# First attention of a two-layer diffusion trunk: the squares' junk row moved to the closing tiles' row, the table of zeros made longer

## Chip, cores, metric

One core of a Trainium2 chip runs the whole program. The metric is the device time of one execution in microseconds (us), the median of several; lower is better. TensorE (PE) multiplies and transposes, VectorE (DVE), ScalarE (ACT) and GpSimd (POOL) do the elementwise work, and the SyncE queue (SP) issues nearly all DMA transfers, one after the other in a fixed order. SBUF is the on-chip memory: 128 partitions; a tile of `[128, 1024]` float32 takes 4096 bytes of each partition.

## What is computed

Two layers over 1024 latent tokens and 256 context tokens of width 1024. Layer 0 has a grouped-query attention and a recurrent mixer side by side, one output projection for both, then a ConvFFN; layer 1 has a neighbourhood attention and a ConvFFN. Cut to the parts that matter here:

```
# layer 0, mixer: q: 8 heads, k and v: 2 heads of 64; latent queries see 256 + 1024 keys, context queries 256
s = einsum("bqhgd,bkhd->bhgqk", q, k) * ATTN_SCALE
o = einsum("bhgqk,bkhd->bqhgd", softmax(s), v)
y = concat([o, readout(recurrent, gate)]) @ w_out            # 1024 x 1024
x = x + g1 * rms_norm(y, norm_post_mix)                      # the closing of a tile
h = rms_norm(x, norm_pre_ffn) * (1 + sc2) + sh2              # input of the ConvFFN
x = x + g2 * rms_norm(conv_ffn(h, w_up, conv_w, conv_b, w_down), norm_post_ffn)

def rms_norm(x, w): return x * rsqrt(mean(x * x) + EPS) * w
```

Everything is float32; a product is made of three matmuls of split operands (high and low parts, the `h`/`hi` and `l`/`lo` tiles).

## The kernel before

**The stage of the change** is `even_attention` (639 to 1061 us of the span): the attention, and in its gaps the output projection `project()`, which makes ten tiles of 128 tokens: two of the context, then eight latent ones. Its tiles live in the pool `at`, which lays them out from its bottom upward in the order in which they are first asked for: `zeros` (a column of zeros, 256 bytes), `pv_t` (1024 bytes), `sq_junk` (1024 bytes), the context keys `K2_0c`, three query tiles `a_q`, and so on; `y`, `y_x` and last of all `yjunk` (1024 bytes) lie at its top.

**The closing of a tile** is a list of small steps (`late`), of which one is taken after each group of three matmuls, or one after the other when no matmuls are left. For each half of the tile `y_half` (L351) squares the projection's PSUM bank on ACT, for the sum of squares alone (the squares themselves go into the junk row `yjunk` and are never read), and copies the bank to `y` on DVE. Then come `y_rstd` (DVE, DVE, POOL), `y_norm` and the sum with the old token values `y_x` (L1222, DVE), the store of `y` to `x1d` (L1224), `squares` (L1191: two ACT squares into the junk row `sq_junk`, again for the sums alone), another `y_rstd`, the scaling of `y` into `y_x` (L1229, ACT) and its store to `xnd` (L1230, issued by POOL). The old values for the next tile are loaded by L1216.

**The next stage** is the first ConvFFN's front (`up_front` in `ffn_up`, L1611 and on). SP there issues ten loads `n_x<-xnd` (512 KB each): the two context tiles, latent tiles 0 to 3, then two loads of the up-projection's weights (`w_raw<-in_w_up`, L1530), then latent tiles 4 to 7. The first `n_x` lies at the bottom of a new pool over the first 4096 bytes of `at`, and so over `zeros`, `pv_t`, `sq_junk`, `K2_0c` and the first `a_q`; the second and third lie above it. PE then transposes (L1344: eight context steps of two, then eight steps of four for tiles 0 to 3, later eight for tiles 4 to 7), ACT scales each step's bank (L1345, into `n_t` for the context and `x_t` after), and DVE splits the result (L1332 the high part, L1333 the low part). Between the sixth and the seventh context step ACT and POOL split the first block of weights (`w_A11h`, L1546, and `w_A11l`, L1547); after the eighth the second (`w_A12h`).

**What sets the order**: ACT, DVE, POOL, PE and SP keep the order in which the code stands (`in_order`), across both stages. SP stops at a load whose place in SBUF is still in use, and all loads behind it stand still too. A tile of a later pool waits for every instruction that used the bytes under it.

Of the kernel before, what the change touches and what calls it, by code (L numbers as in the profile page):

```python
# [11 lines left out]
F32 = mybir.dt.float32  # L12
F32R = mybir.dt.float32r
BF16 = mybir.dt.bfloat16
AF = mybir.ActivationFunctionType
# [5 lines left out]
P = 128  # L21
# [18 lines left out]
LINE = 32  # L40
# [25 lines left out]
class Trunk:  # L66
# [958 lines left out]
    def even_attention(self, gp, tp, pp, sp):  # L1025
# [5 lines left out]
        nc, a = self.nc, self.a  # L1031
# [155 lines left out]
                st["ready"] = b  # L1187

        def squares(y, ms):
            for h in range(2):  # L1190
                nc.scalar.activation(yjunk, y[:, 512 * h:512 * h + 512], AF.Square, scale=1.0 / 32.0, accum_out=ms[:, h:h + 1])  # L1191

        late = []

# [49 lines left out]
                elif late:  # L1244
                    late.pop(0)()

        zeros = sp.tile([P, 2 * LINE], F32, name="zeros", bufs=1)[:, 0:1]
        nc.vector.memset(zeros, 0.0)
        pv_t = sp.tile([P, QB], F32, name="pv_t", bufs=1)
        yjunk = sp.tile([P, 512], BF16, name="sq_junk", bufs=1)  # L1250
        N = 2 * len(pairs)
        later = {4: lambda: load_keys(0, 0), 6: lambda: load_keys(0, 1), 8: lambda: load_values(0, NT - 2),
                 10: lambda: load_keys(1, 0), 12: lambda: load_keys(1, 1), 14: lambda: load_gate(1)}
# [1614 lines left out]
```

## Time and profile before

| | us |
|---|---|
| median of 3 runs | 3322.68 |
| lowest, highest | 3320.38, 3323.68 |
| the profiled execution | 3321.63 |
| its span | 3319.9 |

The profile is one execution. Its page gives busy time by engine and the chain of work that ended last; the timeline gives single instructions with their start, their duration and, in brackets, how long the engine had been idle and for whom it waited. `SPq` marks the issue of a DMA by SP, `ACT`, `DVE`, `PE` and `POOL` the engines, `PEld` the weight loads of PE. In a row of windows stand the busy time of each engine, the clock that was granted to PE (PEclk, 1.00 is full), the mean share of time in which the DMA engines were busy, and the bytes moved.

### The profile page before, as it was taken

To read this page: it belongs to the slowest core of one execution; us is meant where nothing else is said; L and a number is where in the kernel's file an instruction comes from. 1 tells how busy PE (TensorE), PEld (TensorE's weight loads), DVE (VectorE), ACT (ScalarE), POOL (GpSimd) and SP (SyncE) were. 2 spreads that over 40 slices of the span, in tenths; PEclk is the share of its full clock that TensorE was granted. 3 is DMA by queue.
4 is the path that set the end of the run, shared out by engine and by line. 5 is a ranking of instruction groups with operands and counts; after the bars stand their busy time and mean duration, and the time that the engine had idled before them with its cause. 6 is when DMAs were issued, how large, how long until landed. Compare 5 with 4: busy or idle time off the path is not lost.

```text
span 3319.9 us, 48782 instructions
## 1 busy us (share of the span) xinstructions
PE 3097.1 (93%) x18364; PEld 2547.6 (77%) x18364; DVE 2019.6 (61%) x3386; ACT 1502.2 (45%) x2681; POOL 1562.5 (47%) x1181
## 2 busy tenths in 40 slices
PE   7989999789997899999999989999998989999997
PEld 4766777478886688888878768898986768888785
DVE  4366666567774654554577862477775555555778
ACT  3232232366664543343344442566665434434443
POOL 1130111487773566666510111677764367777202
PEclk8999999889998899999999989999998989999998
DMA  6534311721114121211385772222224212222856
GB/s 249 197 103 133 119 49 38 271 73 60 48 61 153 41 76 69 75 67 66 108 288 195 264 229 107 73 63 61 63 81 155 90 64 88 84 77 89 281 179 218
DMA packets 203357, 398.73 MB, mean 120 GB/s; under 512 B 23521, under 2 KB 85473, under 8 KB 203121
## 3 DMA queue, kind: packets, MB, share of 16 engines
q1 hardware_dynamic: 192512, 358.89, 32.1%
q0 software_dynamic: 10608, 36.72, 2.9%
q8 instruction: 144, 2.36, 0.3%
q14 instruction: 93, 0.75, 0.1%
HBM read 316.86 MB, written 79.06 MB: 119 GB/s over the span
## 4 chain that ended last, share of the span: by engine, by line
PE 72%; DVE 11%; ACT 3%; DMA 3%; issue 3%; POOL 2%; SPq 0%; POOLq 0%; DVEq 0%; ACTq 0%
PE g_ps L136 18%; PE u_g L136 14%; PE d_ps L136 11%; PE u_v L136 10%; PE u_pc L136 4%; PE a_pv L136 2%; PE c_pv L136 2%; PE c_s L136 2%; PE c_pt L2503 2%; PE a_pt L1136 2%; DVE a_pl L1138 1%; PE o_ps L136 1%; PE a_s L136 1%; ACT a_ph L1137 1%; DMA d_rawB<-in_w_down 1%
## 5 line engine op out<-in xcount | busy, mean ns | idle before, releaser
L144 POOL TENSOR_TENSOR rs_r<-rs_e,mhalf 128x1 f32<-128x1 f32 (+3 forms) x106 | 85.7, 809 | 855.7 <-DVE rs_e L143 805.7
L136 PE MATMUL d_ps<-d_Bl,d_Ah 128*128 128x512 f32 x704 | 276.7, 393 | 4.1 <-DVE d_Bl L1874 3.5
L136 PE MATMUL d_ps<-d_Bh,d_Ah 128*128 128x512 f32 x704 | 275.5, 391 | 2.8 <-ACT d_Ah L1873 1.8
L136 PE MATMUL d_ps<-d_Bh,d_Al 128*128 128x512 f32 x704 | 275.7, 392 | 2.0 <-DVE d_Al L1874 1.9
L2486 POOL TENSOR_SCALAR c_p<-c_p,rl 128x640 f32<-128x640 f32 (+1 forms) x128 | 232.5, 1818 | 95.4 <-DVE rl L2485 61.8
L1116 POOL TENSOR_SCALAR a_p<-a_p,rl 128x1280 f32<-128x1280 f32 (+1 forms) x80 | 240.3, 3007 | 55.8 <-DVE rl L1115 49.5
L136 PE MATMUL g_ps<-xh,w_hi 128*128 128x512 f32 (+1 forms) x640 | 256.7, 401 | 5.6 <-DVE hq L748 3.5
L136 PE MATMUL g_ps<-xh,w_lo 128*128 128x512 f32 (+1 forms) x640 | 237.5, 371 | 1.3 <-POOL w_lo L2386 1.3
L136 PE MATMUL g_ps<-xl,w_hi 128*128 128x512 f32 (+1 forms) x640 | 237.7, 371 | 0.0
L1138 DVE TENSOR_TENSOR a_pl<-a_pt,a_ph 128x512 fp32r<-128x512 f32 (+1 forms) x200 | 119.0, 602 | 95.6 <-ACT a_ph L1137 95.5
L1561 DVE TENSOR_TENSOR f_u<-u_v,f_p 128x512 f32<-128x512 f32 x88 | 60.5, 688 | 183.7 <-PE u_v L136 183.7
L1547 POOL TENSOR_TENSOR w_S4l<-w_s,w_S4h 128x512 fp32r<-128x512 f32 x44 | 57.2, 1299 | 229.7 <-ACT w_S4h L1546 229.7
L136 PEld LDWEIGHTS d_ps<-d_Bl,d_Ah 128*128 128x128 f32 x704 | 132.7, 188 | 36.7 <-DVE d_Bl L1874 8.6
L136 PEld LDWEIGHTS d_ps<-d_Bh,d_Ah 128*128 128x128 f32 x704 | 132.8, 189 | 32.6 <-ACT d_Ah L1873 3.1
L136 PEld LDWEIGHTS d_ps<-d_Bh,d_Al 128*128 128x128 f32 x704 | 132.9, 189 | 30.0 <-DVE d_Al L1874 3.3
L1137 ACT CAST a_ph<-a_pt 128x512 fp32r<-128x512 f32 (+1 forms) x200 | 102.0, 518 | 108.6 <-PE a_pt L1136 108.5
L2506 DVE TENSOR_TENSOR c_pl<-c_pt,c_ph 128x256 fp32r<-128x256 f32 (+1 forms) x256 | 112.9, 470 | 57.9 <-ACT c_ph L2505 56.8
L136 PE MATMUL g_ps<-w_hi,xh 128*128 128x512 f32 (+1 forms) x368 | 143.2, 389 | 4.7 <-DVE xh L2260 2.1
L136 PEld LDWEIGHTS g_ps<-xh,w_hi 128*128 128x128 f32 x640 | 121.4, 190 | 31.0 <-issue 14.3
L136 PE MATMUL g_ps<-w_lo,xh 128*128 128x512 f32 (+1 forms) x368 | 137.6, 374 | 4.1 <-DVE w_lo L2247 2.9
L2505 ACT CAST c_ph<-c_pt 128x256 fp32r<-128x256 f32 (+1 forms) x256 | 98.4, 414 | 91.6 <-PE c_pt L2503 89.5
L136 PEld LDWEIGHTS g_ps<-xh,w_lo 128*128 128x128 f32 x640 | 121.0, 189 | 24.1 <-POOL w_lo L2386 1.7
(570 smaller groups left out, 9902.6 us busy)
## 6 DMA issues: line engine op xcount, KB each, us to landing
m_raw<-in_w_mod SPq DMA_DIRECT2D x96, 512.0 KB
w_raw<-in_w_up SPq DMA_DIRECT2D x88, 512.0 KB
d_rawA<-actd SPq DMA_DIRECT2D x77, 512.0 KB
d_rawB<-in_w_down SPq DMA_DIRECT2D x74, 512.0 KB
actd<-f_t SPq DMA_DIRECT2D x22, 640.0 KB
d_t<-in_w_down SPq DMA_DIRECT2D x22, 512.0 KB
actd<-f_t SPq DMA_DIRECT2D x22, 512.0 KB
d_s<-actd SPq DMA_DIRECT2D x20, 512.0 KB
```

Source lines behind the costliest of these rows:

```text
L136: return self.nc.tensor.matmul(out, lhsT, rhs, start=start, stop=stop, skip_group_check=True, **k)
L144: nc.gpsimd.tensor_tensor(out=r[:p, :n], in0=e[:p, :n], in1=self.mhalf[:p, :n], op=OP.pow)
L1116: nc.gpsimd.tensor_scalar(Pt[:, :nk], Pt[:, :nk], rl, None, op0=OP.mult)
L1136: nc.tensor.transpose(pt[:, m, qt * P:(qt + 1) * P], Pt[:, kts[j + m] * P:(kts[j + m] + 1) * P], self.ident)
L1137: nc.scalar.copy(ph[:, j:j + n], pt[:, :n])
L1138: nc.vector.tensor_tensor(out=pl[:, j:j + n], in0=pt[:, :n], in1=ph[:, j:j + n].bitcast(F32), op=OP.subtract)
L1547: nc.gpsimd.tensor_tensor(out=lo, in0=part(j, name), in1=hi.bitcast(F32), op=OP.subtract)
L1561: nc.vector.tensor_tensor(out=out, in0=x, in1=y, op=OP.add)
L2486: nc.gpsimd.tensor_scalar(Pt[:, :n], Pt[:, :n], rl, None, op0=OP.mult)
L2503: nc.tensor.transpose(pt[:, j, :], Pt[:, (src + j) * P:(src + j + 1) * P], self.ident)
L2505: nc.scalar.copy(vap(ph, o, dims), pt[:, :cnt])
L2506: nc.vector.tensor_tensor(out=vap(pl, o, dims), in0=pt[:, :cnt], in1=vap(ph, o, dims).bitcast(F32), op=OP.subtract)
```

## The change

`squares` no longer has a junk row of its own. It asks for a tile named `yjunk` with one buffer, which is the tile that `y_half` uses, at the top of the pool. The tile `sq_junk` is gone (1024 bytes), and `zeros` grows from 256 to 768 bytes, of which only the first column is used, as before. So `pv_t` lies 512 bytes higher than it did and every tile from `K2_0c` on 512 bytes lower. Nothing else differs in the source.

```
         def squares(y, ms):
+            junk = sp.tile([P, 512], BF16, name="yjunk", bufs=1)
             for h in range(2):
-                nc.scalar.activation(yjunk, y[:, 512 * h:512 * h + 512], AF.Square, scale=1.0 / 32.0, accum_out=ms[:, h:h + 1])
+                nc.scalar.activation(junk, y[:, 512 * h:512 * h + 512], AF.Square, scale=1.0 / 32.0, accum_out=ms[:, h:h + 1])
...
-        zeros = sp.tile([P, 2 * LINE], F32, name="zeros", bufs=1)[:, 0:1]
+        zeros = sp.tile([P, 6 * LINE], F32, name="zeros", bufs=1)[:, 0:1]
         nc.vector.memset(zeros, 0.0)
         pv_t = sp.tile([P, QB], F32, name="pv_t", bufs=1)
-        yjunk = sp.tile([P, 512], BF16, name="sq_junk", bufs=1)
```

What it moves shows in the program's rows on two engines. On SP, at the seam of the two stages, the last load of old token values and the first loads of `n_x`, before (the names after "waits" are the semaphores: `DMAHW` and `DMASW` earlier DMAs, the others an engine):

```order
L1216 DMA y_x<-in_x 128x1024 [waits DMAHW7_49,DMASW7_49,Activation_49]
L1611 DMA n_x<-xnd 128x1024 [waits DMAHW0_49,DVE_49,Activation_49]
L1611 DMA n_x<-xnd 128x1024 [waits DMAHW1_49,PE_49]
L1611 DMA n_x<-xnd 128x1024 [waits DMAHW2_49,Pool_49]
L1611 DMA n_x<-xnd 128x1024 [waits DMAHW3_49]
```

and with the change:

```order
L1217 DMA y_x<-in_x 128x1024 [waits DMAHW7_49,DMASW7_49,Activation_49]
L1611 DMA n_x<-xnd 128x1024 [waits DMAHW0_49,DVE_49]
L1611 DMA n_x<-xnd 128x1024 [waits DMAHW1_49,PE_49]
L1611 DMA n_x<-xnd 128x1024 [waits DMAHW2_49,Pool_49]
L1611 DMA n_x<-xnd 128x1024 [waits DMAHW3_49]
```

The order is the same, and the first `n_x` no longer waits for ACT. On ACT, the closing of the last tile (`y_half` twice, then the squares twice, then the scaling), before:

```order
L354 ACTIVATE yjunk,y_ms<-g_ps 128x512 [waits PE_49]
L354 ACTIVATE yjunk,y_ms<-g_ps 128x512 [waits PE_49,Activation_49]
L1191 ACTIVATE sq_junk,y_ms<-y 128x512 [waits DVE_49]
L1191 ACTIVATE sq_junk,y_ms<-y 128x512 [waits Activation_49]
L1229 ACTIVATE y_x<-y,rs_r 128x1024 [waits DMAHW7_49,DMASW7_49,Pool_49]
```

and with the change:

```order
L354 ACTIVATE yjunk,y_ms<-g_ps 128x512 [waits PE_49,Activation_49] x2
L1192 ACTIVATE yjunk,y_ms<-y 128x512 [waits DVE_49,Activation_49]
L1192 ACTIVATE yjunk,y_ms<-y 128x512 [waits Activation_49]
L1230 ACTIVATE y_x<-y,rs_r 128x1024 [waits DMAHW7_49,DMASW7_49,Pool_49]
```

The squares and the first half of a tile now also wait for the ACT instruction that last wrote the shared junk row; over the whole stage nine such waits are added.

## The prediction

> **What bounds the kernel now.** The page comes first: the span, PE's busy share and the chain that ended last.
>
> ```profile
> span 3319.9 us, 48782 instructions
> PE 3097.1 (93%) x18364; PEld 2547.6 (77%) x18364; DVE 2019.6 (61%) x3386; ACT 1502.2 (45%) x2681; POOL 1562.5 (47%) x1181
> PE 72%; DVE 11%; ACT 3%; DMA 3%; issue 3%; POOL 2%; SPq 0%; POOLq 0%; DVEq 0%; ACTq 0%
> ```
>
> PE bounds most of the program; 28% of the chain are seams, where PE stands still for something else. A change that touches only two junk squares per tile and some addresses can matter only at such a seam, so the windows of the attention, of the projection's rest and of the seam behind it come next (us; busy time of PE, PEld, DVE, ACT and POOL with counts; PEclk; DMA share; GB/s):
>
> ```profile
> 639.00:1027.00 388.00, 343.23 (x2124) 294.65 (x2125) 269.08 (x536) 256.90 (x506) 300.94 (x153) 0.96 0.21 72
> 1027.00:1053.00 26.00, 25.76 (x114) 20.99 (x112) 10.05 (x18) 10.48 (x27) 8.64 (x14) 1.00 0.36 135
> 1053.00:1074.00 21.00, 6.37 (x20) 3.21 (x20) 7.78 (x19) 7.26 (x15) 2.37 (x5) 0.59 0.73 265
> ```
>
> From 1027 to 1053 PE is full and the DMA engines are nearly two thirds idle. Then come 21 us in which PE works for 6.4 and the DMA engines are the busy ones. The timeline tells why the transfers come so late:
>
> ```profile
> 1043.18 0.33 SPq L1216 DMA_DIRECT2D y_x<-in_x  x1
> 1058.61 0.63 ACT L1191 ACTIVATE sq_junk<-y 128x512 bf16<-128x512 f32 x1
> 1059.14 0.19 ACT L1191 ACTIVATION_READ_ACCUMULATOR sq_junk<-y 128x1 f32 x1
> 1059.36 3.03 SPq L1611 DMA_DIRECT2D n_x<-xnd  x6
> 1062.49 1.05 SPq L1530 DMA_DIRECT2D w_raw<-in_w_up  x2
> 1063.58 6.88 SPq L1611 DMA_DIRECT2D n_x<-xnd  x4
> ```
>
> SP issues nothing from 1043.51 (1043.18 + 0.33) to 1059.36, and starts 0.03 us after the last square of the last tile has ended (1059.14 + 0.19). The first `n_x` holds a context tile, whose values were written long before; it waits only because it lies over `sq_junk`. ACT shows what this costs:
>
> ```profile
> 1060.45 1.15 ACT L1229 ACTIVATE y_x<-y,rs_r 128x1024 f32<-128x1024 f32 x1 [1.12 <-POOL rs_r L144]
> 1065.23 0.56 ACT L1345 ACTIVATE n_t<-n_pv,mod,mod 128x256 f32<-128x256 f32 x1 [3.63 <-PE n_pv L1344]
> 1065.70 0.56 ACT L1345 ACTIVATE n_t<-n_pc,mod,mod 128x256 f32<-128x256 f32 x1
> 1068.83 0.56 ACT L1345 ACTIVATE n_t<-n_pt,mod,mod 128x256 f32<-128x256 f32 x1
> 1073.16 0.62 ACT L1546 CAST w_A11h<-w_raw 128x512 fp32r<-128x512 f32 x1 [3.77 <-DMA w_raw<-in_w_up]
> 1073.69 0.56 ACT L1345 ACTIVATE n_t<-n_pv,mod,mod 128x256 f32<-128x256 f32 x1
> ```
>
> ACT stands still twice: 3.63 us for the first transposes, which wait for `n_x`, and 3.77 us for the weights, which stand behind six `n_x` in SP's order. The chain from there on has no transfer in it (start, us, what):
>
> ```profile
> 1062.49 10.65 DMA w_raw<-in_w_up
> 1073.69 0.57 ACT n_t L1345
> 1074.28 1.02 DVE x_ctx3h L1332
> ...
> 1085.18 1.58 DVE x_B211l L1333
> ...
> 1086.81 1.81 PE u_g L136 x5
> ```
>
> After 1073.69 DVE's splits set the pace until PE's first long products.
>
> **The change, part by part.** *The wait that goes.* The first `n_x` keeps a wait for DVE, an earlier DMA and, one row on, PE and POOL. Which DVE work lies under it follows from its neighbours, `zeros` and `pv_t`:
>
> ```profile
> L1103 DVE CUSTOM_DVE_ANT_0 a_p<-a_s,zeros x64: 1462/1492/1494, 673.0 to 999.4; 128x1280 f32<-128x1280 f32 x64
> L1172 DVE TENSOR_TENSOR a_oT<-a_pv,pv_t x36: 416/417/419, 653.4 to 1027.3; 64x256 f32<-64x256 f32 x36
> ```
>
> The last reader of `zeros` starts at 999.4 and that of `pv_t` at 1027.3. The attention's PE and POOL work on keys, queries and probabilities is over by then too (its last value product feeds that L1172). So the first `n_x` can go as soon as SP is free, at 1043.5, 15.9 us earlier; six take 3.03 us to issue, until 1046.5.
>
> *Whether they arrive in time.* What the DMA engines move at most, and what else they carry there:
>
> ```profile
> 1070.00:1080.00 10.00, 6.61 (x30) 5.14 (x29) 5.76 (x10) 6.78 (x12) 2.54 (x2) 0.63 1.02 409
> xnd<-y_x POOLq DMA_DIRECT2D x3, 512.0 KB, 3.0
> x1d<-y POOLq DMA_DIRECT2D x2, 512.0 KB, 3.0
> ```
>
> The last two rows are of 1040 to 1085. At 409 GB/s 512 KB (0.524 MB) take 1.28 us, one transfer alone 3.0 from issue to landing. One `y_x`, six `n_x` and at most three stores are ten: 12.8 us, all down by 1056.5. The last `y_x` is the first among them, and the sum that reads it stands behind the last projection product. The two weight loads stay behind that product:
>
> ```profile
> 1052.38 0.39 PE L136 MATMUL g_ps<-w_hi,a_ol 128*128 128x512 f32 x1
> 1063.20 0.45 PE L1344 MATMUL n_pv<-ident,n_x 128*128 128x128 f32 x1 [10.44 <-DMA n_x<-xnd]
> ```
>
> They are issued at 1052.8, with `n_x` 4 and 5 and the last-but-one store about them: five transfers, 6.4 us, plus 3.0: landed by 1062.2 at the worst. The last `n_x` waits for the store of the last tile, as before (the scaling that feeds it ends at 1061.6); it is read only behind the products that began at 1086.81.
>
> *What ACT then does.* PE transposes three context steps into its three free banks while the last tile is closed. ACT, in order, reaches the first one when the scaling ends: 1060.45 + 1.15 = 1061.6. First gain: 3.63 us. Five steps on, at 1068.83 - 3.63 + 0.47 (the spacing of two steps) = 1065.7, it wants the weights, which landed 3.5 us earlier or more. Second gain: 3.77 us. Sum: 7.4; since instructions of ACT that follow each other without a gap overlap by some 0.1 (1065.23 + 0.56 to 1065.70), 7.4 to 7.6. I take 7.5. DVE's splits then start from step seven as in the rows above, at the same distances, and the whole of what follows moves with them.
>
> *Whether it is kept.* Behind the front PE is full and the DMA engines are not, so nothing later holds a fixed time:
>
> ```profile
> 1140.00:1160.00 20.00, 20.00 (x101) 16.98 (x101) 11.16 (x14) 9.47 (x14) 13.28 (x10) 1.00 0.08 34
> 1200.00:1300.00 100.00, 100.00 (x533) 86.61 (x532) 49.07 (x56) 39.67 (x57) 65.53 (x49) 1.00 0.19 69
> ```
>
> *The waits that are added* are between ACT's own instructions, which are in order anyway. The pair L1191 already has such a wait. Nine are added; at 0.2 us each (the accumulator read of 0.19 that would have to end first) they cost 1.8 us of ACT at the most, in a stretch where ACT is busy 10.5 of 26 us and waits for DVE or PE. I take nothing; without that cover only the last tile's two, 0.4 us, would be on the path. *The longer table* is cleared in one column as before and no other row of the stage's start changes: nothing. *The shifted addresses*: the 64 softmax instructions L1103 on six buffers take 1462 to 1494 ns, 2% apart; but those buffers lie 5120 bytes apart, so no row shows a shift of 512. I take nothing, bound by 1% either way over the attention's 388 us, 3.9 us.
>
> The profiled execution: 3321.63 - 7.5 = 3314.1. It stood 1.05 below the median of the runs; the median becomes 3322.68 - 7.5 = **3315.2 us**.
>
> **The rivals.** *A: as worked out*, gain 6.5 to 8.5: 3314.2 to 3316.2.
>
> *B: the clock takes a part back.* PE's granted clock was at half through the gap and rose just before the first products:
>
> ```profile
> 1076.00:1078.00 2.00, 1.82 (x11) 1.59 (x10) 1.93 (x5) 1.97 (x4) 0.56 (x1) 0.65 1.03 412
> 1078.00:1080.00 2.00, 2.00 (x11) 1.56 (x11) 1.97 (x4) 1.97 (x4) 0.00 (x0) 1.00 1.00 377
> 1078.96 0.39 PE L136 MATMUL u_g<-x_B110h,w_A11l 128*128 128x512 f32 x1
> 1079.19 0.39 PE L136 MATMUL u_g<-x_B110h,w_A11h 128*128 128x512 f32 x1
> 1129.64 0.63 PE L136 MATMUL u_v<-x_T40h,w_A22h 128*128 128x512 f32 x1
> 1130.07 0.63 PE L136 MATMUL u_v<-x_T40l,w_A22h 128*128 128x512 f32 x1
> ```
>
> A product starts every 0.23 us at full and every 0.43 at half clock. If the clock rises only after the first twelve, they cost 12 x 0.20 = 2.4 us, and the gain is 5.1: 3317.6. For it: the rise came after about 3 us of dense transposes, which the change moves. Against it: the transposes ahead of them close up too. The Trainium skill (TensorE: Matmul & The Clock Gate, Part 1) says that the clock is judged in free-running windows of about 3.4 us; by that rule the rise may fall up to a window later or earlier, which would make this rival, or its mirror F, a matter of phase. The half clock agrees with the rows; the window no row here can show.
>
> *C: only the first gap closes.* If the weights still came late (SP stopped at one of the rows ahead of them), the gain is 3.6: 3319.1. Against it: 3.5 us to spare.
>
> *D: it doesn't do what it says.* If another wait of the first `n_x` ends as late as the squares, nothing moves: 3322.7. The readers above speak against it.
>
> *E: slower.* The new addresses slow the attention's instructions, which are near PE's pace (343 of 388 us). It turns the sign from 7.5 / 388 = 1.9% on; at 3% it costs 11.6, less the 7.5: 3326.8. The evenness of L1103 speaks against it, as far as it reaches.
>
> *F: more.* A later stretch of half clock (the products at 1129 above are one) closes up with the shift; twelve products at 0.20 bring 2.4 more, two such stretches 4: 3311.2 to 3312.8.
>
> **How the numbers follow.** A 0.67, B 0.12, C 0.07, D 0.04, E 0.05, F 0.05. The predicted time is A's, 3315.2. The range is 3311.2 to 3319.8: it holds A, B, C and F and leaves D and E (0.09) and some scatter out. A measurement of this kernel tells 0.2% from no change, 6.6 us, so 3316.0 is the border. Faster: F and nine tenths of A, 0.65. Same: the rest of A, B, C and D, 0.30. Slower: E, 0.05.
>
> **What would show it.** In the changed profile: six `n_x` issued from about 1043.5, right behind the last `y_x`; the weights at about 1053; the first `n_t` within 0.1 us of the end of the last scaling, at 1061.6; no idle time before `w_A11h`; the products `u_g` that began at 1086.81 at about 1079.3; everything from 1140 on 7.5 us earlier. The attention up to 1027 should stand unmoved within 1 us; if it does not, E or its opposite is at work. A `w_raw` that lands after 1065.7 would make C right, an SP that still waits until 1059 D.

## The result, and the profile after

| kernel | median us | lowest to highest | runs | ratio to before (95%) |
|---|---|---|---|---|
| before | 3323.89 | 3317.06 to 3329.13 | 12 | |
| the change | 3316.61 | 3310.89 to 3321.46 | 12 | 0.9978 (0.9970 to 0.9986) |

The change is faster by 7.3 us (3323.89 - 3316.61), with an interval of 4.7 to 10.0 us (0.0014 and 0.0030 of 3323.89). The forecast was a gain of 7.5. The profiled execution took 3318.7 us. The page's first lines after:

```profile
span 3316.9 us, 48786 instructions
PE 3101.1 (93%) x18364; PEld 2548.8 (77%) x18364; DVE 2018.7 (61%) x3386; ACT 1501.4 (45%) x2681; POOL 1560.2 (47%) x1181
PE 73%; DVE 11%; DMA 3%; ACT 3%; issue 3%; POOL 1%; SPq 0%; DVEq 0%; POOLq 0%; ACTq 0%
```

The two spans differ by only 3.0 us, less than the medians do. Single executions of one kernel lie 10.6 to 12.1 us apart here, so spans of one execution each can't carry the result, and neither can a time of day in the trace. What can be compared is a distance between two landmarks that lie close together. The one used below, called the seam, runs from the start of the last tile's scaling (L1229, now L1230) to the start of the product `u_g<-x_B211l,w_A12h`, the first of the five with which the prediction's chain ended.

The timeline of SP after (start, duration, queue, line, what; a row holds equal issues that follow each other):

```profile
1034.53 11.60 SPq L1217 DMA_DIRECT2D y_x<-in_x  x2
1046.22 2.83 SPq L1611 DMA_DIRECT2D n_x<-xnd  x6
1055.36 0.87 SPq L1530 DMA_DIRECT2D w_raw<-in_w_up  x2
```

The six `n_x` go 0.09 us after the last `y_x` has been issued (1034.53 + 11.60 = 1046.13), no longer after the last square. SP is done with them at 1049.05 and issues the weights at 1055.36, 9.1 us behind the first `n_x`; before it was 3.1 (1062.49 - 1059.36). The timelines of ACT and of PE's first product of the five:

```profile
1063.07 1.15 ACT L1230 ACTIVATE y_x<-y,rs_r 128x1024 f32<-128x1024 f32 x1 [1.11 <-POOL rs_r L144]
1064.13 0.55 ACT L1345 ACTIVATE n_t<-n_pv,mod,mod 128x256 f32<-128x256 f32 x1
...
1067.70 0.56 ACT L1345 ACTIVATE n_t<-n_pt,mod,mod 128x256 f32<-128x256 f32 x1
1068.17 0.61 ACT L1546 CAST w_A11h<-w_raw 128x512 fp32r<-128x512 f32 x1
1068.68 0.56 ACT L1345 ACTIVATE n_t<-n_pv,mod,mod 128x256 f32<-128x256 f32 x1
```

```profile
1064.73 0.69 PE L1344 MATMUL n_pv<-ident,n_x 128*128 128x128 f32 x2 [6.95 <-ACT n_t L1345]
1081.85 0.50 PE L136 MATMUL u_g<-x_B211l,w_A12h 128*128 128x512 f32 x1 [1.17 <-DVE x_B211l L1333]
```

Both idle times of ACT (3.63 and 3.77 us) are gone: the first `n_t` starts as the scaling ends, and `w_A11h` follows the sixth `n_t` without a pause. The seam was 1086.81 - 1060.45 = 26.36 us and is 1081.85 - 1063.07 = 18.78: shorter by 7.58. PE now stands ready with its first context steps and waits 6.95 us for ACT, which is held by the closing of the last tile. The window ahead of the seam (busy time of PE, PEld, DVE, ACT, POOL; PEclk; DMA share; GB/s):

```profile
1046.00:1056.00 10.00, 9.33 (x42) 7.39 (x40) 3.70 (x7) 3.75 (x9) 2.24 (x4) 1.00 0.87 326
```

The transfers that waited behind the last square now lie beside PE's last projection products: a DMA share of 0.87 while PE works 9.33 of 10 us. The chain that ended last has no transfer left at the seam:

```profile
1059.16 1.24 DVE y L1223
...
1063.07 1.15 ACT y_x L1230
1064.22 0.46 ACT n_t L1345
...
1069.28 1.08 DVE x_ctx3h L1332
...
1080.22 1.58 DVE x_B211l L1333
1081.85 1.43 PE u_g L136 x5
```

Where it went through `w_raw` for 10.65 us, it now goes through the last tile's closing and ACT's context steps. That is what is late next.

### The profile page after: what moved, and what is told of

The parts are those of the page before. It is cut to its first block, busy times and chain, and to the rows that moved or that the text cites. A ratio compares the mean times of both kernels' runs of the same rounds, so it can differ in the third digit from the quotient of the medians.

```text
span 3316.9 us, 48786 instructions
## 1 busy us (share of the span) xinstructions
PE 3101.1 (93%) x18364; PEld 2548.8 (77%) x18364; DVE 2018.7 (61%) x3386; ACT 1501.4 (45%) x2681; POOL 1560.2 (47%) x1181
## 4 chain that ended last, share of the span: by engine, by line
PE 73%; DVE 11%; DMA 3%; ACT 3%; issue 3%; POOL 1%; SPq 0%; DVEq 0%; POOLq 0%; ACTq 0%
PE g_ps L136 18%; PE u_g L136 14%; PE d_ps L136 11%; PE u_v L136 11%; PE u_pc L136 4%; PE a_pv L136 2%; PE c_pv L136 2%; PE c_s L136 2%; PE c_pt L2503 2%; PE a_pt L1136 2%; DVE a_pl L1138 1%; PE a_s L136 1%; PE o_ps L136 1%; DMA m_raw<-in_w_mod 1%; ACT a_ph L1137 1%
## 5 line engine op out<-in xcount | busy, mean ns | idle before, releaser
L2486 POOL TENSOR_SCALAR c_p<-c_p,rl 128x640 f32<-128x640 f32 (+1 forms) x128 | 232.2, 1815 | 96.0 <-DVE rl L2485 63.1
```

Source lines behind the costliest of these rows:

```text
L2486: nc.gpsimd.tensor_scalar(Pt[:, :n], Pt[:, :n], rl, None, op0=OP.mult)
```

## The experiments

**The change again.** The same kernel, timed and profiled a second time beside the others.

> The changed kernel once more, beside the others. Wait theory (the first n_x no longer waits for the last squares): 7.5 us faster than before (7.4 of ACT's idle time at the seam), with the six n_x issued right behind the last y_x. Address theory (the tiles' places 512 bytes off make the stage itself faster): 7.5 us faster too, but the attention ends earlier and not the seam. Chance: nothing above 3 us.

Median 3316.37 us over 11 runs, ratio 0.9983 (0.9974 to 0.9991). The span was 3319.0, yet the seam is 1083.84 - 1065.06 = 18.78 us, the same to 0.01. Where no engine waits for a transfer, a seam of one trace can thus be read to a few hundredths of a microsecond, a span only to several. A seam with such waits was not traced twice.

**Wait back: the wait returns, the addresses stay.** On the changed kernel, the squares' junk goes to `pv_t`, which lies at the pool's bottom as `sq_junk` did. No tile moves.

```
         def squares(y, ms):
-            junk = sp.tile([P, 512], BF16, name="yjunk", bufs=1)
+            junk = pv_t.bitcast(BF16)
```

> All tiles lie as in the change, but the squares' junk goes into the bytes of pv_t, which lie under the first n_x: the wait for the last squares is back. Wait theory: the 7.5 us are gone, within 2 us of before; SP issues its first n_x within 0.1 us of the end of the last squares, and ACT is idle some 3.6 us and 3.8 us again. Address theory: 7.5 us faster, as the change.

Median 3321.64, ratio 1.0006 (0.9997 to 1.0016): the gain is gone. SP, ACT and PE of this kernel:

```profile
1064.39 0.19 ACT L1192 ACTIVATION_READ_ACCUMULATOR pv_t<-y 128x1 f32 x1
1064.60 3.19 SPq L1611 DMA_DIRECT2D n_x<-xnd  x6
1065.70 1.15 ACT L1230 ACTIVATE y_x<-y,rs_r 128x1024 f32<-128x1024 f32 x1 [1.12 <-POOL rs_r L144]
1070.38 0.56 ACT L1345 ACTIVATE n_t<-n_pv,mod,mod 128x256 f32<-128x256 f32 x1 [3.53 <-PE n_pv L1344]
1078.74 0.62 ACT L1546 CAST w_A11h<-w_raw 128x512 fp32r<-128x512 f32 x1 [4.20 <-DMA w_raw<-in_w_up]
1092.40 0.50 PE L136 MATMUL u_g<-x_B211l,w_A12h 128*128 128x512 f32 x1 [1.18 <-DVE x_B211l L1333]
```

SP starts 0.02 us after the last square (1064.39 + 0.19) again, and both idle times of ACT are back. The seam is 1092.40 - 1065.70 = 26.70. The wait alone makes the gain; the 512 bytes by which tiles moved make none that shows. That this seam is 0.34 longer than before's lies in the two idle times, which together are 0.33 longer (3.53 + 4.20 against 3.63 + 3.77).

**Sixth waits: round the wait in another way.** On the kernel before, `sq_junk` stays where it was, but the load that lies over it is the sixth in SP's order, not the first; nothing of the attention is touched.

```
-            tags = dict(zip((8, 9, 0, 1, 2, 3, 4, 5, 6, 7), ["x_T" + x for x in ("20h", "20l", "21h", "21l", "30h", "30l")] +
+            tags = dict(zip((8, 9, 0, 1, 2, 3, 4, 5, 6, 7), ["x_T" + x for x in ("20l", "21h", "21l", "30h", "30l", "20h")] +
                             ["x_T1" + x for x in ("0h", "0l", "1h", "1l")]))
+            xs[3] = hp.tile([P, D], F32, name="n_x", tag=tags[3], bufs=1)
...
-                    xs[i] = hp.tile([P, D], F32, name="n_x", tag=t, bufs=1)
+                    if i != 3:
+                        xs[i] = hp.tile([P, D], F32, name="n_x", tag=t, bufs=1)
```

> The kernel before, its junk row at the bottom and all of the attention's addresses untouched; only the first n_x in SP's order and the sixth (latent tile 3) trade places, so that the sixth lies over the junk row and waits for the squares. Wait theory: five n_x are issued behind the last y_x, both of ACT's idle gaps close (the weights are issued about 1060, land by 1064 and are wanted at 1065.7 of the span of before), 6 to 7.5 us faster. Address theory: within 2 us of before.

Median 3315.81, ratio 0.9979 (0.9970 to 0.9988): all of the gain, without the change.

```profile
1051.79 16.07 SPq L1613 DMA_DIRECT2D n_x<-xnd  x6
1067.97 1.15 SPq L1530 DMA_DIRECT2D w_raw<-in_w_up  x2
1068.65 1.15 ACT L1229 ACTIVATE y_x<-y,rs_r 128x1024 f32<-128x1024 f32 x1 [1.12 <-POOL rs_r L144]
...
1073.74 0.61 ACT L1546 CAST w_A11h<-w_raw 128x512 fp32r<-128x512 f32 x1
1087.42 0.50 PE L136 MATMUL u_g<-x_B211l,w_A12h 128*128 128x512 f32 x1 [1.18 <-DVE x_B211l L1333]
```

The row of six issues is 16.07 us long because its last one waits for the squares, and the weights behind it go only at 1067.97, 7.0 us later against the scaling than with the change (0.7 us ahead of it, not 7.7). Still the seam is 18.77. Five loads went ahead of the wait, and the weights are there when ACT gets to them at 1073.74, 5.8 us after their issue; before, they took 10.65 with six `n_x` beside them. The wait for the squares stands unchanged in this kernel and costs nothing: what cost was that six loads and the weights stood behind it together.

**Each gap alone.** *Weights first*, on the kernel before: both weight loads ahead of all ten `n_x`, everything still behind the squares' wait but the weights.

```
             with self.in_order(mybir.EngineType.SP):
+                load(0, 0)
+                load(0, 1)
                 for i, t in tags.items():
-                    if i == 4:
-                        load(0, 0)
-                        load(0, 1)
```

*Weights last*, on the changed kernel: the loads are free of the squares, and the weights go behind all ten `n_x`.

```
                 for i, t in tags.items():
-                    if i == 4:
-                        load(0, 0)
-                        load(0, 1)
                     xs[i] = hp.tile([P, D], F32, name="n_x", tag=t, bufs=1)
                     nc.sync.dma_start(xs[i], self.xnd[i * P:(i + 1) * P])
+                load(0, 0)
+                load(0, 1)
```

Both put the third weight load, `load(1, 0)`, and its pool behind these by hand, so that it keeps its place.

> The kernel before, but the two weight loads stand ahead of the n_x in SP's order, so that they go when PE's last projection product ends (1052.8) while the n_x still wait for the squares. Wait theory, with two gaps of their own: the first gap stays (3.6 us idle before the first n_t), the second (3.77 before w_A11h) closes: 3 to 4 us faster than before. If the two gaps were one and the same wait, 0 or 7.5.

> The change, but the two weight loads stand behind all ten n_x in SP's order, and so behind the last one, which waits for the store of the last tile. Wait theory with two gaps: the first gap stays closed, ACT is idle again before w_A11h, by about 5 us (weights issued some 6.5 us after the last scaling starts, 3 us to land, wanted 5.1 us after it): 2 to 4 us faster than before. If it is the first gap alone that counts, 7.5; if the second alone, nothing.

Weights first: 3319.04, ratio 0.9994 (0.9985 to 1.0003). Weights last: 3319.93, ratio 0.9997 (0.9988 to 1.0006). Neither can be told from no change by its time, and the interval of each holds the gain that its seam shows; the traces are sharper. Weights first:

```profile
1063.45 1.15 ACT L1229 ACTIVATE y_x<-y,rs_r 128x1024 f32<-128x1024 f32 x1 [1.12 <-POOL rs_r L144]
1069.04 0.56 ACT L1345 ACTIVATE n_t<-n_pv,mod,mod 128x256 f32<-128x256 f32 x1 [4.43 <-PE n_pv L1344]
1073.10 0.61 ACT L1546 CAST w_A11h<-w_raw 128x512 fp32r<-128x512 f32 x1
1086.93 0.50 PE L136 MATMUL u_g<-x_B211l,w_A12h 128*128 128x512 f32 x1 [1.18 <-DVE x_B211l L1333]
```

Weights last:

```profile
1060.28 1.15 ACT L1230 ACTIVATE y_x<-y,rs_r 128x1024 f32<-128x1024 f32 x1 [1.12 <-POOL rs_r L144]
1061.34 0.55 ACT L1345 ACTIVATE n_t<-n_pv,mod,mod 128x256 f32<-128x256 f32 x1
1069.80 0.62 ACT L1546 CAST w_A11h<-w_raw 128x512 fp32r<-128x512 f32 x1 [4.32 <-DMA w_raw<-in_w_up]
1083.47 0.51 PE L136 MATMUL u_g<-x_B211l,w_A12h 128*128 128x512 f32 x1 [1.18 <-DVE x_B211l L1333]
```

Each has exactly one of the two idle times: 4.43 us for the first context step, or 4.32 for the weights. The seams are 1086.93 - 1063.45 = 23.48 and 1083.47 - 1060.28 = 23.19, gains of 2.88 and 3.17 against before. Together that is 6.05, less than 7.58, because in either kernel the gap that stays is longer than it was (4.43 against 3.63, 4.32 against 3.77). In weights last that is SP's order: the last `n_x` waits for the last tile's store, and the weights behind it are issued 5.05 us after the scaling's start (1065.33 - 1060.28) and need 4.44 us to land. In weights first PE gets the second context tile 6.16 us after the first `n_x` is issued (1068.52 - 1062.36), where before it took 5.36 (1064.72 - 1059.36); why it lands later was not found.

**Junk only: the junk row moved, the table left short.** On the changed kernel `zeros` goes back to 256 bytes.

```
-        zeros = sp.tile([P, 6 * LINE], F32, name="zeros", bufs=1)[:, 0:1]
+        zeros = sp.tile([P, 2 * LINE], F32, name="zeros", bufs=1)[:, 0:1]
```

> The change without the longer table: the junk row is shared, zeros stays at 256 bytes, and every tile from K2_0c on lies 1024 bytes lower than before, so that K2_0c reaches over the modulation tables that DVE finishes at 637.5 of the span of before; its load then waits for DVE, where it went at 625.6. Wait theory: the seam gains 7.5 as in the change, the start loses some 2 us (the load lands about 3 us after 637.5, so the first scores come at 640.6 and not by 639.6, and the query loads behind it on SP's queue are late too): 4 to 6 us faster than before. If the longer table is worth nothing, 7.5.

Median 3321.31, ratio 0.9992 (0.9983 to 1.0001): by the ratio 2.7 us faster, with an interval from 0.3 slower to 5.6 faster. The seam is that of the change, 1085.06 - 1066.27 = 18.79, so 7.57 us are won there. Part of it is lost where the stage starts:

```profile
639.61 1.26 DVE L339 SCALAR_TENSOR_TENSOR mod<-mod,nrm 128x16 f32<-128x16 f32 x1
640.90 0.38 SPq L1070 DMA_DIRECT2D K_0c<-k2d  x1
...
679.43 1.49 DVE L1103 CUSTOM_DVE_ANT_0 a_p<-a_s,zeros 128x1280 f32<-128x1280 f32 x1
...
1066.27 1.15 ACT L1230 ACTIVATE y_x<-y,rs_r 128x1024 f32<-128x1024 f32 x1 [1.12 <-POOL rs_r L144]
1085.06 0.50 PE L136 MATMUL u_g<-x_B211l,w_A12h 128*128 128x512 f32 x1 [1.18 <-DVE x_B211l L1333]
```

The same rows of the kernel before:

```profile
625.56 0.42 SPq L1070 DMA_DIRECT2D K_0c<-k2d  x1
636.13 1.41 DVE L339 SCALAR_TENSOR_TENSOR mod<-mod,nrm 128x16 f32<-128x16 f32 x1
...
672.99 1.49 DVE L1103 CUSTOM_DVE_ANT_0 a_p<-a_s,zeros 128x1280 f32<-128x1280 f32 x1 [1.03 <-PE a_s L136]
```

The load of the first keys used to be issued 10.57 us ahead of L339, the last instruction of the modulation. Now it goes 0.03 us after L339 has ended (639.61 + 1.26). With 1024 bytes less at the bottom, `K2_0c` begins at byte 21376 of a partition, and the modulation's tiles end at 21696; with the change it begins at 21888. In the built program the load waits for DVE in this kernel, and neither before nor with the change. From L339 to the first long softmax instruction the kernel before takes 36.86 us, this one 39.82: 3.0 us lost. In the six other runs it is 36.7 to 37.2 us, so the loss is known to some tenths. The net, 7.57 - 2.96 = 4.6, lies inside the interval of the medians, which alone would not tell it from no change. The longer table is thus no part of the gain; it keeps the freed bytes from opening the same kind of wait at the stage's other end.

**Not tried.** What is late now is the closing of the last tile, ahead of ACT's context steps; `xnd` of that tile is needed only much later. Putting the context steps ahead of the closing would use PE's 6.95 us, but both stages would need their SBUF and PSUM at once, and no kernel of that kind was run.

## Why the prediction was right

**The wait that goes.** Right: the six loads follow the last `y_x` by 0.09 us. Wait back shows that the squares' junk was what held them, so D (it doesn't do what it says) is out. The issue came at 1046.22, 16.85 us ahead of the scaling where the prediction had 1060.45 - 1043.5 = 16.95; the trace as a whole stood later.

**Whether they arrive.** Right: neither ACT nor PE waits for a transfer from the scaling to the five products. The weights were issued 1063.07 - 1055.36 = 7.7 us ahead of the scaling, as forecast (1060.45 - 1052.8 = 7.65). The trace's landing records put the first weights at 1061.6, and ACT takes them at 1068.17: 6.5 us to spare, so C (only the first gap closes) was further off than the forecast 3.5 us said. The step ahead of that was a little short: the sixth `n_x` landed at 1059.9, where the forecast had all ten transfers down by 1056.5, which is 1059.1 in this trace (its scaling starts 2.62 us later). Nothing waited for it. In sixth waits the weights landed 0.7 us before ACT took them, and that was still in time.

**What ACT then does.** Right in both terms and in the sum: 7.4 to 7.6 forecast for the seam, 7.58 measured, 7.3 (4.7 to 10.0) in the medians. The two gaps as separate terms held only because both closed; a gap that is left alone grows by 0.6 to 0.8 us, as the pair of experiments shows.

**Whether it is kept.** The medians keep it. From the scaling to the first store of the next part (`actd`) the trace of the change gains more than 7.58:

```profile
L1595 SPq DMA_DIRECT2D actd<-f_t x1: 326/326/326, 1143.8 to 1143.8; - x1
```

That is 80.73 us after the scaling; before it was 89.45 (1149.9 - 1060.45). So 8.7 us by then, 1.1 more than at the product. This 1.1 is not the removed wait's. Wait back, which has the wait, takes 62.0 us from the product to the store (1154.4 - 1092.40), like the change (1143.8 - 1081.85); before took 63.1. In the trace of before PE's granted clock was 0.50 from 1088 to 1090, right behind the product, and the five products took 1.81 us; in the change and in wait back it was 1.00 there, and they took 1.43. So F (more) is not shown as an effect of the change: the half clock was absent with the wait as well.

**The rival B was priced without its cover.** In the changed kernel's trace the clock rose before the first product, as before. In wait back it did not:

```profile
1085.28 0.63 PE L136 MATMUL u_g<-x_B110h,w_A11l 128*128 128x512 f32 x1
1085.71 0.52 PE L136 MATMUL u_g<-x_B110h,w_A11h 128*128 128x512 f32 x1
1086.07 0.39 PE L136 MATMUL u_g<-x_B110l,w_A11h 128*128 128x512 f32 x1
```

The third and fourth product start 0.43 us apart (1085.28 to 1085.71) where 0.23 is the distance at full clock; only from 1086.07 on does one take 0.39 again. Weights last has four slow products too. They delay PE by about 0.8 us (4 x 0.20), and at the seam's end they cost nothing: from `w_A11h` to the product `u_g<-x_B211l` it is 13.66 us in wait back (1092.40 - 1078.74) and 13.67 in weights last, against 13.65 before and 13.68 in the change. DVE's splits, which set the pace at full clock, cover the delay. But that cover was used up. In wait back the chain that ended last runs through PE's twelve products:

```profile
1084.63 3.44 PE u_g L136 x12
```

From there it goes over ACT's `x_t` to the split `x_B211h`, where in the change it stays on DVE's splits. So only a third of what B supposed was seen, four slow products of twelve, and that was just covered. What twelve would have cost no run shows.

**What was costed at nothing.** The nine added waits of ACT cost nothing that shows:

```profile
1060.48 0.63 ACT L1192 ACTIVATE yjunk<-y 128x512 bf16<-128x512 f32 x1 [4.37 <-DVE y L1223]
1061.23 0.63 ACT L1192 ACTIVATE yjunk<-y 128x512 bf16<-128x512 f32 x1
```

The two squares start 0.75 us apart, as before (1057.86 and 1058.61). The shifted addresses cost nothing either: the 64 long softmax instructions keep their pace,

```profile
L1103 DVE CUSTOM_DVE_ANT_0 a_p<-a_s,zeros x64: 1464/1492/1493, 676.1 to 1002.0; 128x1280 f32<-128x1280 f32 x64
L1172 DVE TENSOR_TENSOR a_oT<-a_pv,pv_t x36: 416/417/420, 656.3 to 1029.9; 64x256 f32<-64x256 f32 x36
```

and from the first of them to the last reader of `pv_t` the attention takes 1029.9 - 676.1 = 353.8 us, against 1027.3 - 673.0 = 354.3. That ends E. The longer table was rightly costed at nothing against the kernel before. The prediction did not ask what would have happened without it: 3.0 us.

**What it called for and did not get**: an attention that stands still within 1 us up to 1027, and everything from 1140 on 7.5 us earlier. This trace runs 3.0 us late at the end of the modulation and 2.6 at the last scaling, ahead of anything that the change shortens, and its lead over the trace of before shrinks to 3.0 us at the end. As tests these were badly chosen, since they compare times of day in two executions; the distances hold.

## What to carry to other kernels

In a program like this one a load on an in-order queue waits for whatever last used the bytes it lands on, and all loads behind it wait too; so look for scratch that is written late and lies under the next stage's first load, and move the scratch, or put that load later in the queue. The price of such a wait isn't its length (16 us here) but the idle time of the engines that the crowded transfers cause behind it (7.6 us). When scratch is freed, everything above it slides: check what each moved tile now lies on.

## What the runs showed of the hardware

Executions of one kernel scatter by 10 to 13 us, while the changed kernel's seam repeats to 0.01 us in two traces. Part of the scatter lies ahead of the stage, in code that is the same in all kernels. The modulation's L336 before and after (count, durations in ns, first and last start):

```profile
L336 DVE TENSOR_TENSOR mod<-mod_pt,bmt x2: 158/162/165, 616.3 to 635.9; 128x16 f32<-128x16 f32 x2
```

```profile
L336 DVE TENSOR_TENSOR mod<-mod_pt,bmt x2: 159/162/166, 618.1 to 638.9; 128x16 f32<-128x16 f32 x2
```

The last one starts at 635.9 and 638.9, and in the change run again at 641.8. What causes it stays open.

The moment at which PE's clock rises against the work before it is not fixed. From the first timeline row of four transposes (L1344) on, PE was busy nearly without a pause; the rise came 2.4 us behind it in sixth waits (1073.90 to 1076.3), 4.7 in the change (1068.32 to 1073.0) and 6.1 in wait back (1079.87 to 1086.0). In the change (us; busy times; PEclk; DMA share; GB/s):

```profile
1072.00:1073.00 1.00, 0.99 (x6) 0.59 (x4) 0.93 (x4) 1.00 (x3) 0.00 (x0) 0.50 0.13 39
1073.00:1074.00 1.00, 1.00 (x7) 0.86 (x7) 1.00 (x2) 0.97 (x2) 0.00 (x0) 0.98 1.06 141
```

A spread of 3.7 us is near the window in the rule that the prediction took from the Trainium skill (TensorE: Matmul & The Clock Gate, Part 1), by which the clock is judged in free-running windows of about 3.4 us. The runs show the spread, not the window. The shortest rise, 2.4 us, is less than one such window; by that rule PE's thinner work ahead of the row (0.68 to 1.00 of each microsecond from 1070 on in sixth waits) would have to count too, which no run tests.
